# Hybrid decoder trunk: lambda's softplus joined to the decay's log, modulation steps and gated-output splits spread, output-projection weights put into the ordered slots

## Chip, core and metric

The kernel runs on one NeuronCore of one Trainium2 chip. TensorE (PE) does the matrix products, VectorE (DVE), ScalarE (ACT) and GpSimd (POOL) the element-wise work, and SyncE (SP) issues most DMA transfers. The metric is the device time of one execution in microseconds (us).

## What is computed

A trunk of two layers runs over one sequence of 1024 positions of width 1024, in float32. Every layer is `x + gate(c) * mixer(rmsnorm(x) * (1 + scale(c)) + shift(c))`, and a norm follows the last.

```python
mod = c_act @ ada_w[layer] + ada_b[layer]          # shift, scale, gate
# layer 0
log_f = jax.nn.log_sigmoid((f_logit + b_f).astype(jnp.float32))
b_out = forgetting_attention(b_q, b_k, b_v, log_f)  # logits + cumulative log decay
y = jnp.concatenate([a_out, b_out], axis=-1) * jax.nn.silu(gate)
return y @ w_out
# layer 1
log_a = -LRU_C * r * jax.nn.softplus(-lam.astype(jnp.float32))
a = jnp.exp(log_a)
u = jnp.sqrt(-jnp.expm1(2.0 * log_a)) * (i * xc.astype(jnp.float32))
# h_t = a_t h_(t-1) + u_t along the sequence
y = jnp.transpose(hs, (1, 0, 2)).astype(h.dtype) * jax.nn.silu(gate)
return y @ w_out
```

`a_out` is a sliding-window attention of 8 heads; r and i are sigmoids of block-diagonal products of xc, the causal convolution of the first half of the input projection.

## The kernel before

Activations lie transposed: 8 tiles of 128 channels (KT = 8), and two halves of 512 positions, h0 and h1. A float32 product is taken as three products of rounded parts, so every operand is split: `copy` (line 103) rounds it on ACT, and `sub` (112) takes the rest on DVE or POOL. A product of one output tile by one half is a group of 24 matmuls with 512 columns. `split` and `half_of` do this for weights: ACT rounds (whi), POOL takes the rest (wlo).

**Order.** A scheduler may move instructions on an engine unless its name is in the set `ordered` (lines 73 to 97): then they are kept as the code is written. An engine works through its instructions in order, so one that waits holds up those behind it, and SP's transfers behave in the same way.

**Start, gates, modulation.** `squares` makes the norm's sums. `log1p_exp_neg_abs` (153) is the log(1 + exp(-abs(z))) of a softplus or a log-sigmoid; it needs ACT's exp and log tables. The modulation vector is made by 32 steps in the gate loop and after it: `mod_steps` (541) runs one `mod_dot`, an instruction on DVE over 128x1024 numbers of `ada`, and `fetch` loads the following pieces. Pieces come as pairs in a buffer V or alone in a buffer P (line 526).

**V and decay.** The loop over tb (from 614) makes the V tiles of both attentions (`va`, `vb`) and the forget logits `fz`, in PSUM banks that alternate between two pools of two. Then `lf`, the log decay, is made; `sp` and `nsp` are made from lambda by a chain of its own (lines 638 to 643). The first fill (k and q projections of attention A: ak_0, aq_0) follows, with `decay()` (648) at its 48th matmul: it scans `lf` (`loc`) and writes the decays to memory (`gd`). A fill's group is `ps_fill` in a pool of two banks; `use_k` and `use_q` empty it, each half by copies on ACT and subtractions on DVE (`kla`, `aq`).

**Attention.** `weave` (1059) interleaves the units' instructions (scores sA, sB; transposes ptA, ptB, split into pth and ptl; products oA, oB) with a fill of projections for a later unit. In the last fill but one, `then_split` (1125) makes `drip` call `split_act` (1113) six times, which splits the gated outputs gy into yh (ACT) and yl (DVE for odd tiles, POOL for even). They are the operands of layer 0's output projection, the fill after that.

**Layer 1.** `slot(c)` (1422) handles channel tile c: `gates(c)` makes psr and psi, four groups of three matmuls; ACT makes r, i, th, a; DVE the products and the scan hs; then `proj1` of lx_(c+2) for h0 and h1 and of lg_c for h0 and h1, 24 matmuls each. `gate_a` and `gate_b` make y1 = silu(lg) * hs and its split. `split_xc` and `split_r` split the operands of the next slot's gates (xch, xcl; wrh, wrl). `load_next` and `split_next` feed the weights of lx and lg in the order of use; everything here is in program order.

**Output projection.** Behind the slots `ordered` is cleared (1468), and three stretches of positions (512, 256, 256) are multiplied by 8 weight tiles wo. In the first stretch, groups e = 0 to 2 leave out the last input tile until y1 of it is there (AHEAD = 3). Loads and splits of wo stand in the loop over e, and so does the load of x (`xn`, from `x1d`).

Of the kernel before, what the change touches and what calls it, by code (L numbers as in the profile page):

```python
# [48 lines left out]
def hybrid_trunk(  # L49
# [472 lines left out]


    chunks, ndone = {}, [0]
    units = collections.deque()
    for m in range(0, 32, 4):
        units += [(m, m + 1), (m + 2,), (m + 3,)] if m < 24 else [(m + i,) for i in range(4)]
    held = {1: 0, 2: 0}

    def fetch():  # L530

        while units and held[len(units[0])] < 3 - len(units[0]):
            u = units.popleft()
            n = len(u)
            held[n] += 1
            t = at.tile([P, 2, S], F32, tag="V", name=f"ada_{u[0]}") if n == 2 else t4("P", f"ada_{u[0]}").unsqueeze(1)
            sync.dma_start(t, ada[:, u[0] : u[0] + n])
            for i, m in enumerate(u):
                chunks[m] = t[:, i], n if i + 1 == n else 0

    def mod_steps(n):
        for _ in range(min(n, 32 - ndone[0])):
            m = ndone[0]
            lay, c0 = ((0, 16), (1, 0), (1, 8), (1, 16))[m // KT]
            j = c0 + m % KT
            t, n = chunks.pop(m)
            ab = C_AB0 + 24 * lay + j
            mod_dot(t, crow, lay, j, col[:, ab : ab + 1])
            ndone[0] += 1
            if n:  # L550
                held[n] -= 1
            fetch()

    NV = 264
# [59 lines left out]
    z = at.tile([P, NB, 8], F32, tag="fz", name="fz", bufs=1)  # L614
# [20 lines left out]
    lf = at.tile([P, NB, 8], F32, tag="lf", name="lf", bufs=1)  # L635
    log1p_exp_neg_abs(lf, z, at, [P, NB, 8], "sp")
    dve.scalar_tensor_tensor(out=lf, in0=z, scalar=0.0, in1=lf, op0=ALU.min, op1=ALU.subtract)

    sp, nl, nsp = (const.tile([P, KT], F32, name=n) for n in ("sp", "nl", "nsp"))
    lam = col[:, C_LAM : C_LAM + 8]  # L640
    log1p_exp_neg_abs(sp, lam, const, [P, KT], "lm")
    dve.tensor_scalar(out=nl, in0=lam, scalar1=-1.0, scalar2=0.0, op0=ALU.mult, op1=ALU.max)
    add(dve, sp, sp, nl)
    dve.tensor_scalar(out=nsp, in0=sp, scalar1=-8.0, scalar2=None, op0=ALU.mult)
    dve.tensor_scalar(out=sp, in0=sp, scalar1=8.0, scalar2=None, op0=ALU.mult)
    gd = dram.tile([8, NB, S], F32, name="gd")

    def decay():
# [297 lines left out]
    def fill(jobs, ahead=lambda: None):  # L946
# [3 lines left out]
        for n, (_, ks, xs, use) in enumerate(jobs):  # L950
# [5 lines left out]
            for h, (xhi, xlo) in xs().items():  # L956
                ps = ps_mm(f"ps_fill_{h}")
                cnt = 0
                for k in ks:
                    whi, wlo = w[k]  # L960
                    for i, (a, b) in enumerate(((whi, xhi), (wlo, xhi), (whi, xlo))):
                        mm(ps, a, b[:, k], start=(k == ks[0] and i == 0), stop=(k == ks[-1] and i == 2))
                        cnt += 1
                        if late and cnt == 9:
                            late.pop()()
                        if drip and cnt % 4 == 0:
                            drip.popleft()()
                        yield MM
                x = use(h, ps)
# [143 lines left out]
    def split_act(ti, h):  # L1113
# [11 lines left out]
    def then_split(job):  # L1125

        weights, ks, xs, use = job
# [6 lines left out]
        return weights, ks, xs, use_and_split  # L1134

    def residual(xn, ps, lay, e):
        dve.scalar_tensor_tensor(
# [27 lines left out]

    o0 = [o0_job(e) for e in range(KT)]
    jobs.append(o0)
    jobs[7][-1] = then_split(jobs[7][-1])
# [148 lines left out]
    halves = collections.deque((ti, i, name) for ti, name in jobs_l for i in range(2))  # L1317
    raws, ready = collections.deque(), collections.deque()

    def load_next():  # L1320
        if halves:
            ti, i, name = halves.popleft()
            raws.append((load_w(wl[ti][:, 4 * i : 4 * i + 4], [P, 4, P], f"{name}_{i}"), f"{name}_{i}"))

    def split_next():
        if raws:
            w = []
            for _ in range(2):
                w += half_of(raws.popleft())
                load_next()  # L1330
            ready.append(w)

    def rt(tag, c, dt=F32, w=S, bufs=1):
        return rp.tile([P, w], dt, tag=tag, name=f"{tag}_r{c}", bufs=bufs)
# [60 lines left out]
    def gate_a(c, h):  # L1395
# [1 line left out]
        sg = sgs[c, h] = rp.tile([P, HALF], F32, tag="sg", name=f"sg_r{c}_{h}", bufs=2)  # L1397
        act.activation(sg, lgs[c, h], AF.Sigmoid)
        mul(dve, sg, lgs[c, h], sg)
        mul(gp, sg, sg, hss[c][:, half(h)])  # L1400

    def gate_b(c, h):
        sg = sgs.pop((c, h))
        copy(y1h[:, c, half(h)], sg)
        sub(gp, y1l[:, c, half(h)], sg, r32(y1h[:, c, half(h)]))

    lgs, sgs = {}, {}
    ordered |= ALL
# [4 lines left out]
        conv(c, 0, ps01[c])()  # L1413
    split_xc(0, half(0))
    split_r(0)
    taps = conv(0, 1, proj1(0, "lx_0", 1, w01[0]))
    split_next()
    taps()
# [2 lines left out]

    def slot(c):
        n = c + 2
        ps = gates(c)
        if c:
            gate_a(c - 1, 1)
# [14 lines left out]
        w = ready.popleft()  # L1441
        split_next()
        if n < KT:
            taps = conv(n, 0, proj1(0, f"lx_{n}", 0, w))
        act.activation(a2, a_, AF.Square)
        if n < KT:
            taps()
# [17 lines left out]
        slot(c)  # L1465
    gate_a(KT - 1, 1)
    gate_b(KT - 1, 1)
    ordered.clear()
    l1.close()


    xp = ctx.enter_context(tc.tile_pool(name="xp1", bufs=2, reuse_waits="tile"))
    wout = []
    for t0, tw in ((0, 512), (512, 256), (768, 256)):
        h, o = t0 // HALF, t0 % HALF
        ts = slice(t0, t0 + tw)
        xn = xp.tile([P, KT, tw], F32, tag="xn", name=f"x2_{t0}")
        sqa = xp.tile([P, tw], F32, tag="sqa", name=f"sqa2_{t0}")
        late_ = []
        for e in range(KT):  # L1480
            if t0 == 0:
                if e % 4 == 1:
                    wr = [hl.tile([P, 4, KT, P], F32R, tag=f"hl{e // 4 * 2 + i}", name=f"wo1_{e}_{i}") for i in range(2)]
                    for c in range(4):
                        wout.append([(wr[0][:, c, k], wr[1][:, c, k]) for k in range(KT)])
                if e == 0:
                    wout.append(load_tile(wo1[0], "wo1_0"))
                else:
                    for c in range(2):
                        raw = load_w(wo1[e][:, 4 * c : 4 * c + 4], [P, 4, P], f"wo1_{e}_{c}")  # L1490
                        split(raw, *(t[:, (e - 1) % 4, 4 * c : 4 * c + 4] for t in wr))
            w = wout[e]
            sync.dma_start(xn[:, e], x1d[:, h, e, o : o + tw])
            ps = ps_1(f"ps_o1_{t0}_{e}")
# [5 lines left out]
            for e_, w_, ps in late_:  # L1500
# [3 lines left out]
                if t0 < 768 or e_ + 1 < KT:  # L1504
                    square_sum(sqa, xn[:, e_], e_, xp, f"o1_{t0}")
            late_ = []
        sqs = [sqa]
        if t0 == 768:
            sqs.append(xp.tile([P, tw], F32, tag="sq", name=f"sq7_{t0}", bufs=2))
# [84 lines left out]
```

## Time and profile before

| | |
|---|---|
| median of 3 runs | 895.16 us (893.98 to 898.52) |
| profiled execution | 896.32 us, span 894.5 us |
| mean granted TensorE clock | 0.986 |
| PE matmuls | 4618 records, 862.2 us busy |
| DVE, ACT, POOL busy | 563.4, 537.6 and 378.3 us |

The span runs from the first instruction to the last; the rest of the execution's time lies around it. A profile counts an engine as busy while it has an instruction in hand. "Idle before" is the time in which the engine had nothing to run before an instruction, and the releaser is what it waited for. Matmuls of 512 columns start 0.23 us apart although each shows 0.39 us, since they overlap.

### The profile page before, as it was taken

The numbers are of one execution on the slowest core, as the hardware profiler recorded it, in microseconds if no ns is written. First come the engines' busy times: TensorE is split into PE (matmuls) and PEld (weight loads), VectorE is DVE, ScalarE is ACT, GpSimd is POOL, SyncE is SP. The second block draws the span as 40 slices with busy tenths as digits, with TensorE's granted clock in tenths as the row PEclk, the third lists the DMA queues.
The fourth block names the chain that finished last, engine by engine and source line by source line (L and its number), as shares of the span: only waits on it lengthen the run. The fifth ranks groups of instructions, "written<-read, shape, count | busy, mean of one in ns | idle before, by whom it ended". The sixth has DMA issues, their size and how long they took to land.

```text
span 894.5 us, 13516 instructions
## 1 busy us (share of the span) xinstructions
PE 862.2 (96%) x4618; PEld 731.6 (82%) x4618; DVE 563.4 (63%) x1143; ACT 537.6 (60%) x1051; POOL 378.3 (42%) x428
## 2 busy tenths in 40 slices
PE   8999989999999999999999999999999999998995
PEld 8887888888878888888778888877888888777995
DVE  6976797688676566666656768376555566423353
ACT  5756124688676566665666647358767666764332
POOL 3843342343352232331554645532456555773000
PEclk8999999999999999999999999999999999999998
DMA  9933884100113223322463564412111111134042
GB/s 347 414 135 142 263 307 124 42 25 25 36 42 113 88 93 112 121 86 78 132 204 112 176 195 147 140 36 64 43 54 39 44 54 54 48 106 165 3 152 82
DMA packets 54333, 103.83 MB, mean 116 GB/s; under 512 B 6929, under 2 KB 20689, under 8 KB 53497
## 3 DMA queue, kind: packets, MB, share of 16 engines
q1 hardware_dynamic: 53112, 101.93, 34.0%
q10 hardware_dynamic: 1152, 1.05, 0.5%
q8 instruction: 36, 0.59, 0.3%
q14 instruction: 33, 0.26, 0.1%
HBM read 94.02 MB, written 8.93 MB: 115 GB/s over the span
## 4 chain that ended last, share of the span: by engine, by line
PE 62%; DVE 12%; ACT 11%; issue 5%; POOL 4%; DMA 4%; SPq 0%; DVEq 0%; POOLq 0%; ACTq 0%
PE ps_fill L85 21%; PE ps_o L85 8%; PE ps_o0c L85 5%; PE pst L85 5%; PE oB L85 4%; PE ptB L85 3%; PE sB L85 3%; DVE xc_r L85 3%; DMA ada<-in_ada_dram 2%; DVE hs_r L85 2%; PE ps_lx L85 2%; DVE ada L85 2%; PE sA L85 2%; PE oA L85 1%; PE ptA L85 1%
## 5 line engine op out<-in xcount | busy, mean ns | idle before, releaser
L85 PE MATMUL ps_o<-y1h,wo 128*128 128x256 f32 (+1 forms) x336 | 76.3, 323 | 3.9 <-DVE x L85 2.7
L85 DVE TENSOR_TENSOR ptl_B<-ptB,pth_B 128x512 fp32r<-128x512 f32 (+1 forms) x80 | 50.8, 635 | 39.5 <-ACT pth_B L85 39.2
L85 ACT ACTIVATE pth_B<-ptB 128x512 fp32r<-128x512 f32 (+1 forms) x80 | 44.1, 551 | 47.6 <-PE ptB L85 47.4
L85 ACT ACTIVATE pB<-pB,mnB 128x128 f32<-128x128 f32 (+3 forms) x64 | 49.5, 774 | 31.1 <-DVE mnB L85 25.7
L85 PEld LDWEIGHTS ps_o<-y1h,wo 128*128 128x128 f32 x336 | 56.6, 193 | 9.3 <-DVE x L85 3.1
L85 POOL TENSOR_SCALAR_AFFINE_SELECT pB<-pB 128x128 f32<-128x128 f32 x64 | 19.2, 303 | 94.8 <-DMA pB<-gd 84.1
L85 PE MATMUL pst<-hh,ws 128*128 128x512 f32 x192 | 55.3, 396 | 0.0
L85 PE MATMUL ps_o<-y1l,wo 128*128 128x256 f32 (+1 forms) x168 | 53.9, 323 | 0.0
L85 PE MATMUL ps_lx<-h1l,whi_lx 128*128 128x512 f32 x128 | 50.4, 394 | 0.2 <-POOL h1l L85 0.2
L85 PE MATMUL ps_lx<-h1h,whi_lx 128*128 128x512 f32 x128 | 50.5, 395 | 0.0
L85 PE MATMUL ps_lx<-h1h,wlo_lx 128*128 128x512 f32 x128 | 50.3, 393 | 0.0
L85 DVE CUSTOM_DVE_ANT_0 ada<-ada,crow,col 128x1024 f32<-128x1024 f32 x32 | 46.0, 1465 | 6.9 <-DMA ada<-in_ada_dram 6.9
L85 DVE SCALAR_TENSOR_TENSOR xc_r<-ps_lx,col,xc_r 128x509 f32<-128x509 f32 (+2 forms) x48 | 35.6, 744 | 23.2 <-ACT xt_r L85 22.1
L85 PE MATMUL ps_lg<-h1h,whi_lg 128*128 128x512 f32 x128 | 49.8, 389 | 0.0
L85 PE MATMUL ps_lg<-h1l,whi_lg 128*128 128x512 f32 x128 | 49.8, 389 | 0.0
L85 PE MATMUL ps_lg<-h1h,wlo_lg 128*128 128x512 f32 x128 | 49.8, 389 | 0.0
L85 ACT ACT_TABLE_LOAD x37 | 47.5, 1283 | 2.6 <-DVE sq_pth L85 0.9
L85 PE MATMUL ptB<-ident,pB 128*128 128x128 f32 x288 | 45.9, 276 | 3.0 <-DVE gy L85 1.2
L85 PEld LDWEIGHTS ptB<-ident,pB 128*128 128x128 f32 x288 | 35.9, 141 | 14.8 <-ACT pB L85 2.5
L85 DVE CUSTOM_DVE_ANT_0 pB<-sB,pB 128x384 f32<-128x384 f32 (+2 forms) x64 | 35.4, 554 | 17.4 <-PE sB L85 8.2
L85 ACT ACTIVATE sq_o<-x 128x512 f32<-128x512 f32 (+1 forms) x33 | 17.9, 545 | 42.0 <-DVE x L85 41.7
L85 PEld LDWEIGHTS pst<-hh,ws 128*128 128x128 f32 x192 | 35.9, 188 | 8.7 <-issue 0.6
(317 smaller groups left out, 2826.8 us busy)
## 6 DMA issues: line engine op xcount, KB each, us to landing
ada<-in_ada_dram SPq DMA_DIRECT2D x36, 512.0 KB
ada<-in_ada_dram SPq DMA_DIRECT2D x6, 1024.0 KB
x<-in_xT_dram SPq DMA_DIRECT2D x20, 256.0 KB
pB<-gd SPq DMA_DIRECT2D x8, 512.0 KB
raw_o0a<-in_wo_dram SPq DMA_DIRECT2D x16, 256.0 KB
raw_o0c<-in_wo_dram SPq DMA_DIRECT2D x16, 256.0 KB
x1d<-x SPq DMA_DIRECT2D x16, 256.0 KB
raw_lx<-in_wl_dram SPq DMA_DIRECT2D x16, 256.0 KB
```

The lines of the kernel that those rows point to most:

```text
L85: ins = issue(*args, **kw)
```

## The change

Six things are changed.

1. lambda becomes a ninth block of the forget logits (`z[:, NB]`), and `sp` and `nsp` are taken from `lf`'s ninth block. Its own chain goes.
2. Modulation: steps in the gates of h1 become 2 per tile (1 at the last) from 3, in the V stage 1 per block from 1 or 2, and eight steps go into the first fill, one every 12 matmuls. DVE is kept in program order through the V stage and that fill. Pairs end at m = 16.
3. Splits of gated outputs: `drip` fires every 8 matmuls from every 4, the jobs of that fill are arranged q, v(h0), k with the splits, v(h1), and all yl of h0 are made on POOL.
4. lx_2's h0 goes ahead of `gates(0)`.
5. `split_r` of the next slot moves up behind `split_xc`, with its load a slot earlier.
6. Output projection: its weights join the lists of `load_next`; wo_0 and wo_1 are split in slot 7, wo_2 behind the last y1, wo_(e+3) in step e; x is loaded before the loop; e = 0 to 3 use the gates' PSUM banks; tile 7's products and y1l are made on DVE.

```diff
-            if i < 7:
-                mod_steps(3)
+            mod_steps(2 if i < 7 else 1)
...
-    ordered.add("pe")
+    ordered |= {"pe", "dve"}
...
+    z = at.tile([P, NB + 1, 8], F32, tag="fz", name="fz", bufs=1)
+    lam = col[:, C_LAM : C_LAM + 8]
+    gp.tensor_copy(z[:, NB], lam)
...
-        mod_steps(1 + tb % 2)
+        mod_steps(1)
...
-    log1p_exp_neg_abs(sp, lam, const, [P, KT], "lm")
...
+    dve.tensor_scalar(out=nsp, in0=lf[:, NB], scalar1=8.0, scalar2=None, op0=ALU.mult)
+    dve.tensor_scalar(out=sp, in0=lf[:, NB], scalar1=-8.0, scalar2=None, op0=ALU.mult)
...
-                        if drip and cnt % 4 == 0:
+                        if drip and cnt % 8 == 0:
...
+        if n % 12 == 8:
+            mod_steps(1)
+    ordered.discard("dve")
...
-        sub(dve if ti % 2 else gp, yl[h][:, ti], gy[h][:, ti], r32(yh[h][:, ti]))
+        sub(dve if ti % 2 and h else gp, yl[h][:, ti], gy[h][:, ti], r32(yh[h][:, ti]))
...
+        return [jq, part(0), (weights, ks, xs, use_and_split), part(1)]
...
+    jobs_l = [(wl[ti], name) for ti, name in jobs_l] + [(wo1[e], f"wo1_{e}") for e in range(KT)]
...
+    def split_out(e):
...
+        for c in range(2):
+            split(raws.popleft()[0], *(t[:, n % 4, 4 * c : 4 * c + 4] for t in wr))
+            load_next()
...
-        mul(gp, sg, sg, hss[c][:, half(h)])
+        mul(gp if c + 1 < KT else dve, sg, sg, hss[c][:, half(h)])
...
+        if c == 0:
+            w = ready.popleft()
+            ps_x = proj1(0, f"lx_{n}", 0, w)
         ps = gates(c)
...
-            load_r(c + 1)
             split_xc(c + 1)
+            split_r(c + 1)
+            if c + 2 < KT:
+                load_r(c + 2)
...
-        if c + 1 < KT:
-            split_r(c + 1)
+        elif c == KT - 1:
+            wout.append(ready.popleft())
+            split_out(1)
...
+        for e in range(KT):
+            sync.dma_start(xn[:, e], x1d[:, h, e, o : o + tw])
+        if t0 == 0:
+            split_out(2)
...
+            if t0 == 0 and e + 3 < KT:
+                split_out(e + 3)
...
+            ps = (ps_s, ps_t)[e % 2](nm) if t0 == 0 and e <= AHEAD else ps_1(nm)
```

How this stands on two engines is shown at two places.

On DVE, near the end of the first fill, before: `loc` are the decay's scans, `kla` and `aq` the subtractions that empty a fill's bank, and `pA` the first softmax.

```order
204 L85 TENSOR_SCALAR loc<-loc 8x256
205 L85 TENSOR_TENSOR kla_1321<-ps_fill_1379,kha_1319 64x512
206 L85 CAST kha_1319<-kha_1319 64x512
207 L85 TENSOR_SCALAR loc<-loc 8x384
208 L85 TENSOR_SCALAR loc<-loc 8x512
209 L85 TENSOR_SCALAR loc<-loc 8x640
210 L85 TENSOR_SCALAR loc<-loc 8x768
211 L85 TENSOR_SCALAR loc<-loc 8x896
212 L85 SCALAR_TENSOR_TENSOR aq_0_1484<-ps_fill_1424,aq_0_1484 64x512
213 L85 SCALAR_TENSOR_TENSOR aq_1_1485<-ps_fill_1424,aq_1_1485 64x512
214 L85 SCALAR_TENSOR_TENSOR aq_0_1484<-ps_fill_1490,aq_0_1484 64x512
```

The same place on DVE after the change; `ada` with `mod` is a modulation step.

```order
189 L85 TENSOR_SCALAR loc<-loc 8x640
190 L85 TENSOR_SCALAR loc<-loc 8x768
191 L85 TENSOR_SCALAR loc<-loc 8x896
192 L85 ISA ada_1364,mod<-ada_1364,crow,col 128x1024
193 L85 ISA mod 128x1
194 L85 SCALAR_TENSOR_TENSOR gsc<-mod,col 128x8
195 L85 ISA ada_1379,mod<-ada_1379,crow,col 128x1024
196 L85 ISA mod 128x1
197 L85 SCALAR_TENSOR_TENSOR aq_0_1470<-ps_fill_1404,aq_0_1470 64x512
198 L85 SCALAR_TENSOR_TENSOR aq_1_1471<-ps_fill_1404,aq_1_1471 64x512
199 L85 ISA ada_1449,mod<-ada_1449,crow,col 128x1024
200 L85 ISA mod 128x1
```

All `loc` now stand behind the last `kla`, and two modulation steps stand ahead of the first pair of `aq`, two ahead of the second. Four more steps stand further up, between and ahead of the `kla`.

On ACT, at the end of layer 1, before: `a_r` and `th_r` belong to slot 7, `wo` are the output projection's weights, `sg_r` the gates of tile 7.

```order
820 L85 ACTIVATE a_r_8163<-r_r_8156,nsp 128x1024
821 L85 ACTIVATE wo_1_0_8279<-raw_wo_1_0_8281 128x512
822 L85 ACTIVATE wo_1_0_8279<-raw_wo_1_1_8285 128x512
823 L85 ACTIVATE wo_1_0_8279<-raw_wo_2_0_8312 128x512
824 L85 ACTIVATE a_r_8164<-a_r_8163 128x1024
825 L85 ACTIVATE wo_1_0_8279<-raw_wo_2_1_8316 128x512
826 L85 ACT_TABLE_LOAD
827 L85 ACTIVATE th_r_8162<-th_r_8162,tiny 128x1024
828 L85 ACT_TABLE_LOAD
829 L85 ACTIVATE sg_r_0_8201<-ps_lg_0_8176 128x512
830 L85 ACTIVATE wo_1_0_8279<-raw_wo_3_0_8362 128x512
831 L85 ACTIVATE wo_1_0_8279<-raw_wo_3_1_8366 128x512
```

And after the change.

```order
817 L85 ACTIVATE a_r_8157<-r_r_8150,nsp 128x1024
818 L85 ACTIVATE whi_wo_0_0_8164<-raw_wo_0_0_7956 128x512
819 L85 ACTIVATE whi_wo_0_1_8170<-raw_wo_0_1_8060 128x512
820 L85 ACTIVATE a_r_8158<-a_r_8157 128x1024
821 L85 ACT_TABLE_LOAD
822 L85 ACTIVATE th_r_8156<-th_r_8156,tiny 128x1024
823 L85 ACTIVATE wo_1_0_8182<-raw_wo_1_0_8066 128x512
824 L85 ACTIVATE wo_1_0_8182<-raw_wo_1_1_8168 128x512
825 L85 ACT_TABLE_LOAD
826 L85 ACTIVATE sg_r_0_8217<-ps_lg_0_8192 128x512
827 L85 ACTIVATE y1h<-sg_r_0_8217 128x512
828 L85 ACTIVATE sg_r_1_8248<-ps_lg_1_8223 128x512
```

`wo_0` now stands in slot 7 where `wo_1` stood, `wo_1` behind the square root of slot 7, and `wo_2` behind the last y1h, where before the first half of it came ahead of the square of `a_r`.

More of the change, by code (lines that the diff above doesn't have):

```diff
@@ L524, in hybrid_trunk @@
     chunks, ndone = {}, [0]
-    units = collections.deque()
+    blocks = collections.deque()
     for m in range(0, 32, 4):
-        units += [(m, m + 1), (m + 2,), (m + 3,)] if m < 24 else [(m + i,) for i in range(4)]
-    held = {1: 0, 2: 0}
+        blocks += [(m, m + 1), (m + 2,), (m + 3,)] if m < 16 else [(m + i,) for i in range(4)]
+    room = {1: 0, 2: 0}
     def fetch():
-        while units and held[len(units[0])] < 3 - len(units[0]):
-            u = units.popleft()
+        while blocks and room[len(blocks[0])] < 3 - len(blocks[0]):
+            u = blocks.popleft()
             n = len(u)
-            held[n] += 1
+            room[n] += 1
             t = at.tile([P, 2, S], F32, tag="V", name=f"ada_{u[0]}") if n == 2 else t4("P", f"ada_{u[0]}").unsqueeze(1)
@@ L1122, in split_act, with then_split @@
         copy(yh[h][:, ti], gy[h][:, ti])
-        sub(dve if ti % 2 else gp, yl[h][:, ti], gy[h][:, ti], r32(yh[h][:, ti]))
-    def then_split(job):
-        weights, ks, xs, use = job
+        sub(dve if ti % 2 and h else gp, yl[h][:, ti], gy[h][:, ti], r32(yh[h][:, ti]))
+    def then_split(jq, jv, jk):
+        weights, ks, xs, use = jk
         def use_and_split(h, ps):
@@ L1132, in use_and_split, with part @@
                 drip.extend(lambda ti=ti: split_act(ti, 0) for ti in range(KT - 2))
-        return weights, ks, xs, use_and_split
+        def part(h):
+            return (*jv[:2], lambda: {h: (hh[h], hlo[h])}, jv[3])
+        return [jq, part(0), (weights, ks, xs, use_and_split), part(1)]
     def residual(xn, ps, lay, e):
@@ L1316, in hybrid_trunk @@
         jobs_l += [(c + 2, f"lx_{c + 2}")] * (c + 2 < KT) + [(8 + c, f"lg_{c}")]
-    halves = collections.deque((ti, i, name) for ti, name in jobs_l for i in range(2))
+    jobs_l = [(wl[ti], name) for ti, name in jobs_l] + [(wo1[e], f"wo1_{e}") for e in range(KT)]
+    halves = collections.deque((src, i, name) for src, name in jobs_l for i in range(2))
     raws, ready = collections.deque(), collections.deque()
@@ L1321, in load_next @@
         if halves:
-            ti, i, name = halves.popleft()
-            raws.append((load_w(wl[ti][:, 4 * i : 4 * i + 4], [P, 4, P], f"{name}_{i}"), f"{name}_{i}"))
+            src, i, name = halves.popleft()
+            raws.append((load_w(src[:, 4 * i : 4 * i + 4], [P, 4, P], f"{name}_{i}"), f"{name}_{i}"))
     def split_next():
[L1326 to L1331, printed above, removed]
+        w = []
+        for _ in range(2):
+            w += half_of(raws.popleft())
+            load_next()
+        ready.append(w)
+    wout, wr = [], []
+    def split_out(e):
+        n = e - 1
+        if n % 4 == 0:
+            wr[:] = [hl.tile([P, 4, KT, P], F32R, tag=f"hl{n // 4 * 2 + i}", name=f"wo1_{e}_{i}") for i in range(2)]
+        for c in range(2):
+            split(raws.popleft()[0], *(t[:, n % 4, 4 * c : 4 * c + 4] for t in wr))
+            load_next()
+        wout.append([(wr[0][:, n % 4, k], wr[1][:, n % 4, k]) for k in range(KT)])
     def rt(tag, c, dt=F32, w=S, bufs=1):
@@ L1404, in gate_b @@
         copy(y1h[:, c, half(h)], sg)
-        sub(gp, y1l[:, c, half(h)], sg, r32(y1h[:, c, half(h)]))
+        sub(gp if c + 1 < KT else dve, y1l[:, c, half(h)], sg, r32(y1h[:, c, half(h)]))
     lgs, sgs = {}, {}
@@ L1440, in slot @@
         act.activation(a_, r, AF.Exp, scale=nsp[:, c : c + 1])
-        w = ready.popleft()
+        if c:
+            w = ready.popleft()
         split_next()
         if n < KT:
-            taps = conv(n, 0, proj1(0, f"lx_{n}", 0, w))
+            taps = conv(n, 0, proj1(0, f"lx_{n}", 0, w) if c else ps_x)
         act.activation(a2, a_, AF.Square)
@@ L1478, in hybrid_trunk @@
         sqa = xp.tile([P, tw], F32, tag="sqa", name=f"sqa2_{t0}")
+        for e in range(KT):
+            sync.dma_start(xn[:, e], x1d[:, h, e, o : o + tw])
+        if t0 == 0:
+            split_out(2)
         late_ = []
         for e in range(KT):
[L1481 to L1491, printed above, removed]
+            if t0 == 0 and e + 3 < KT:
+                split_out(e + 3)
             w = wout[e]
-            sync.dma_start(xn[:, e], x1d[:, h, e, o : o + tw])
-            ps = ps_1(f"ps_o1_{t0}_{e}")
+            nm = f"ps_o1_{t0}_{e}"
+            ps = (ps_s, ps_t)[e % 2](nm) if t0 == 0 and e <= AHEAD else ps_1(nm)
             last = KT - 1 if t0 == 0 and e < AHEAD else KT
@@ L1506, in hybrid_trunk @@
             late_ = []
+        ordered.clear()
         sqs = [sqa]
```

19 lines of the change are left out of this document (6 added, 13 removed).

## Prediction

> **What bounds the kernel now.** I read the page first, for the busy shares of the engines.
>
> ```profile
> PE 862.2 (96%) x4618; PEld 731.6 (82%) x4618; DVE 563.4 (63%) x1143; ACT 537.6 (60%) x1051; POOL 378.3 (42%) x428
> ```
>
> PE is busy for 96% of the span, and the change neither adds nor removes a matmul. What can be won is therefore PE's idle time and the stretches in which its clock is halved. The waits, with PE as the one who waits, say where that idle time is (total, times, longest):
>
> ```profile
> PE oB L85 <- DVE ptl_B L85: 2.8, 3, 1.6
> PE ps_o L85 <- DVE x L85: 2.7, 1, 2.7
> ...
> PE psr L85 <- ACT xch_r L85: 1.9, 1, 1.9
> PE ps_v L85 <- DVE fz L85: 1.4, 1, 1.4
> ...
> PE ps_v L85 <- POOL wvl L85: 1.1, 1, 1.1
> ...
> PE psr L85 <- POOL wrl_r L85: 0.9, 1, 0.9
> PE psi L85 <- POOL wrl_r L85: 0.7, 1, 0.7
> ```
>
> No wait dominates: the largest is 2.8 us in three pieces. The stretches show what the clock takes besides (length, busy time of the engines, granted clock, DMA share, GB/s):
>
> ```profile
> 10.00:20.00 10.00, 10.00 (x61) 9.91 (x61) 8.31 (x18) 3.39 (x7) 2.51 (x2) 0.66 1.01 386
> 120.00:130.00 10.00, 8.57 (x71) 8.39 (x70) 10.00 (x19) 2.66 (x7) 5.62 (x3) 1.00 0.78 248
> 440.00:450.00 10.00, 8.38 (x41) 6.92 (x41) 7.06 (x17) 5.20 (x11) 3.80 (x8) 0.83 0.06 15
> 600.00:610.00 10.00, 8.12 (x29) 5.96 (x28) 8.18 (x16) 6.55 (x10) 3.54 (x4) 0.85 0.23 66
> 810.00:820.00 10.00, 7.93 (x29) 6.45 (x30) 5.58 (x8) 5.50 (x9) 2.38 (x2) 0.83 0.88 305
> ```
>
> Behind the waits of 1.6 (oB), 1.9 (psr) and 2.7 us (ps_o) the clock falls to 0.83, 0.85 and 0.83 for ten us, which costs 1.7, 1.5 and 1.7 us more; behind the 1.4 us of ps_v it stays at 1.00. So I price an idle stretch of over about 1.6 us at itself plus 1.7. The Trainium skill, "TensorE: Matmul & The Clock Gate", section "Why this matters for your kernels", asks only for no gap of over about 3 us; the three rows speak against it, since shorter gaps were followed by the lower clock, and what it would make of the sum stands with the rivals.
>
> **Start-up.** The softplus of lambda leaves ScalarE's start; its eight columns ride in the decay's log.
>
> ```profile
> 3.38 1.28 ACT L85 ACT_TABLE_LOAD   x1
> 4.68 0.21 ACT L85 ACTIVATE lm<-lm 128x8 f32<-128x8 f32 x1
> 4.91 1.28 ACT L85 ACT_TABLE_LOAD   x1
> ```
>
> Two table loads of 1.28 go, 2.6 us in which the squares of the norm waited. They can't all be won: the DMA is full (1.01 from 10 to 20), the squares need x, and a clock of 0.66 in that stretch is there whether the work starts early or late. Ends 0 and -2.6; I take -1.7, nearer to the loads. What is added (one copy on GpSimd, eight columns more on a 64-column chain) is hidden: GpSimd is 42% busy.
>
> **Modulation steps and the V stage.** DVE is busy for all of 120 to 130, and the writes of va, vb and fz stand behind steps such as this:
>
> ```profile
> 121.52 2.30 DVE L85 CUSTOM_DVE_ANT_0 ada<-ada,crow,col 128x1024 f32<-128x1024 f32 x1
> ```
>
> With fewer steps in the gates and one per V block, the two ps_v waits go: -2.5. But eight steps now lie in the fill of ak and aq, and DVE's order is now the program's there. This is what DVE did in that stretch (138 to 161; busy, mean ns, idle before and releaser), and the last read of a fill's bank:
>
> ```profile
> L85 DVE TENSOR_TENSOR_SCAN loc<-ones,lfT 8x128 f32<-8x128 f32 x8 | 3.3, 411 | 1.0 <-PE lfT L85 0.9
> L85 DVE TENSOR_TENSOR kla<-ps_fill,kha 64x512 fp32r<-64x512 f32 x4 | 2.7, 681 | 1.3 <-ACT kha L85 1.3
> L85 DVE CUSTOM_DVE_ANT_0 ada<-ada,crow,col 128x1024 f32<-128x1024 f32 x2 | 2.6, 1284 | 0.8 <-DMA ada<-in_ada_dram 0.8
> L85 DVE SCALAR_TENSOR_TENSOR aq<-ps_fill,aq 64x512 fp32r<-64x512 f32 x2 | 1.4, 690 | 0.7 <-ACT aq L85 0.7
> ```
>
> ```profile
> 160.32 0.69 DVE L85 SCALAR_TENSOR_TENSOR aq<-ps_fill,aq 64x512 fp32r<-64x512 f32 x1 [0.66 <-ACT aq L85]
> ```
>
> ```profile
> 161.16 0.47 PE L85 MATMUL ps_fill<-hh,whi_aq 128*128 128x512 f32 x1
> ```
>
> The aq subtraction ends at 161.01, and PE begins the next fill, which takes the same bank, at 161.16: no slack already. In the new order six more steps (the moved ones 24 to 29) stand ahead of that subtraction, as do all scans and all TENSOR_SCALARs of loc. Six by 1.28 is 7.7 us; of this DVE can put 1.0 + 1.3 + 0.8 + 0.7 = 3.8 into its old idle times. So PE waits 3.9 us, and 1.7 for the clock: +5.6. Ends: 0, if DVE leaves the V stage so much earlier that it catches up, and 7.7 + 1.7. Queued behind are loc's writes, and on SP the last two ada loads behind those. Together -2.5 + 5.6 = +3.1.
>
> **Splits of the gated outputs.** The burst before PE's 1.6 us of oB:
>
> ```profile
> L85 ACT ACTIVATE yh<-gy x6: 619/623/624, 434.8 to 437.8; 128x512 fp32r<-128x512 f32 x6
> L85 POOL TENSOR_TENSOR yl<-gy,yh x2: 1293/1521/1749, 435.5 to 436.7; 128x512 fp32r<-128x512 f32 x2
> L85 DVE TENSOR_TENSOR yl<-gy,yh x2: 1315/1342/1370, 435.9 to 437.7; 128x512 fp32r<-128x512 f32 x2
> ```
>
> The two of about 1.34 on DVE go to GpSimd, where the row says 1.29 to 1.75, so they are no slower there and free DVE. The six copies on ACT stay in one place: four, one khb, two, and only then the pth_B that PE wants next. Ends: the 1.6 + 1.7 goes (-3.3), or ACT's 3.7 us of copies keep as long a wait (0). I take -1.2, nearer to staying. A later subtraction of the same kind, which moves off DVE ahead of the third, 1.0 us wait of oB (2.8 less 1.6 is what the other two hold), gives 0 to -1.0: -0.5.
>
> **Layer 1 and the output projection.** These edits meet in ScalarE's chain, so I follow that.
>
> ```profile
> 603.02 0.40 PE L85 MATMUL psr<-xch_r,wrh_r 128*128 128x512 f32 x1
> ```
>
> ```profile
> 607.69 1.26 ACT L85 ACTIVATE r_r<-psr,col 128x512 f32<-128x512 f32 x2
> ```
>
> ```profile
> 614.54 1.14 ACT L85 ACTIVATE whi_lg<-raw_lg 128x512 fp32r<-128x512 f32 x2
> ```
>
> ```profile
> 615.29 1.29 POOL L85 TENSOR_TENSOR wlo_lg<-raw_lg,whi_lg 128x512 fp32r<-128x512 f32 x1 [11.23 <-issue]
> ```
>
> ```profile
> 746.54 0.50 ACT L85 ACTIVATE wrh_r<-wr_r 128x128 fp32r<-128x128 f32 x2
> ```
>
> A group of 24 products in these rows takes 24 x 0.23 = 5.5 us. With lx_2's first half ahead of the gates, PE fills its 1.9 us (and the clock's 1.5), but the first psr ends at 603.0 + 5.5 + 0.7 = 609.2, so r_r comes 1.7 late. With 0.4 of wrh now ahead of it, whi_lg comes at 616.7 and GpSimd's first half of wlo_lg ends at 615.29 + 1.29 + 2.1 = 618.7; PE wants it at 603.0 + 5.5 + 2.7 + 5.5 = 616.7. Of the 3.4 removed 2.0 come back at once. From then on ScalarE's loop of a slot is longer by about 0.3 (the 0.4, with 0.1 of slack), and over six slots it takes the rest; the 0.9 + 0.7 of the weights' low halves goes (-1.6).
>
> ```profile
> 783.58 1.66 ACT L85 ACTIVATE wo<-raw_wo 128x512 fp32r<-128x512 f32 x3
> ```
>
> ```profile
> 784.68 0.39 PE L85 MATMUL ps_o<-y1h,whi_wo 128*128 128x512 f32 x1
> ```
>
> ```profile
> 812.07 0.80 PE L85 MATMUL ps_o<-y1h,wo 128*128 128x512 f32 x1 [2.72 <-DVE x L85]
> ```
>
> ```profile
> 792.64 2.29 DVE L85 TENSOR_TENSOR_SCAN hs_r<-a_r,i_r 128x1024 f32<-128x1024 f32 x1
> ```
>
> ```profile
> 811.26 2.12 DVE L85 SCALAR_TENSOR_TENSOR x<-ps_o,mod,x 128x512 f32<-128x512 f32 x3 [8.46 <-DMA x<-x1d]
> ```
>
> wo_0 is now split where wo_1 was: 783.6, plus 1.7 + 0.4 + 1.7 of lag, less about 2 since GpSimd's part of wo_0 no longer stands ahead of the gate of the slot before: about 785.6. A copy and GpSimd's 1.29 later, at 787.5, the first low half is there. PE is ready at 784.7 - 1.6 = 783.1, so it waits 4.4 us. wo_2 comes in ScalarE's order only behind the last y1h. The last scan ended at 794.9 and I leave it there (the lag against the three wo copies that no longer stand ahead of it); sigmoids, two products and y1h of both halves then take about 4 us and wo_2's copy and low half 1.9: about 800.6, and till then the third group waits. From there 21, 24 and 9 products (12.4 us) end at 813.0. Before, the fifth group began at 812.1, at half clock (1.7): worth 813.8. x is loaded early, so the 2.7 us wait for it goes, as does its clock. Layer 1 and the projection: -0.8; ends -7 (3.4 + 1.6 + 4.4 gone, 2.0 back, ScalarE doesn't lag) and +4 (the low clock behind both new waits).
>
> **Sum.** -1.7 + 3.1 - 1.2 - 0.5 - 0.8 = -1.1. The profiled execution took 896.32 us (span 894.5 and 1.8 around it), 1.2 above the median of 895.16. So 895.2 by it, and 894.0 as a median.
>
> **The rivals.** One: the removed waits go and nothing takes their place. Then 2.6 + 2.5 + 3.3 + 1.0 + 3.4 + 1.6 + 4.4 = 18.8 go, 876.4. Against it: the aq bank without slack. If that wait alone stays out, it is 894.0 - 5.6 = 888.4, so this case spans 876 to 889. For it: DVE idles in the fill, and it gets there with less behind it.
>
> Two, on the slower side: DVE, in program order, blocks the fill for longer. If all eight steps cost 2.30, as beside GpSimd at 121.52, and each waits for its load for 0.4, as two did for 0.8, this adds 8 x 1.02 + 3.2 = 11.4: 905.4. It decides the sign from a wait of about 9.5 at the bank, 5.6 over mine. For it: two buffers hold all that is loaded ahead, and SP has loc's writes ahead of the last loads. Against: GpSimd is busy for 42% of the span, so most steps would not run beside it.
>
> Three: the clock doesn't follow from short waits. Then the 1.7 given to oB's and the projection's gaps isn't won, and the sum is -1.1 + 1.7 + 1.7 = +2.3, a median of 897.4. This is what the rule of the Trainium skill's page above would give, since only the 3.9 us at the bank is over its bound.
>
> **How the numbers follow.** The forecast has 0.45, with 889 to 899 of its own; the first rival 0.30, the second 0.18, the third 0.07. A measurement of this kernel tells about 0.5% from no change, 890.7 and 899.6. Faster: 0.28 of the first rival and 0.09 of the forecast, 0.37. Slower: 0.18 + 0.04 + 0.02 = 0.24. The same: 0.39. The range leaves out the ends of the first two rivals: 880 to 902.
>
> **What would show it.** The fill: PE waiting for aq by 3 to 5 us near 160, with DVE at a modulation step; without that wait the forecast is too slow. ScalarE's first squares come over 2 us earlier, and PE has no ps_v wait. In layer 1 a wait of ps_lg for wlo_lg near 617, none of psr for xch_r, and near 782 and 798 waits of ps_o for wo's low halves where there was one for x. If ps_o waits for nothing, ScalarE's lag was wrong.

## The result, and the profile after

The changed kernel takes 908.25 us (median of 4 runs, 906.54 to 911.03), the kernel before 895.23 us (4 runs, 893.98 to 898.52). The ratio is 1.0143, with an interval of 1.0105 to 1.018: slower, where no change was forecast, and above the range. The profiled execution of the changed kernel took 907.82 us, with a span of 905.7 us, 11.2 more than before, and a mean granted clock of 0.977.

The busy shares of the engines after the change, from the page:

```profile
PE 867.2 (96%) x4618; PEld 735.4 (81%) x4618; DVE 564.4 (62%) x1134; ACT 535.0 (59%) x1047; POOL 372.7 (41%) x429
```

This row shows nothing of what happened: every engine has as much work as before, within 1.5%. The waits of PE after the change (total, times, longest) show it:

```profile
PE ps_fill L85 <- DVE aq L85: 6.5, 1, 6.5
PE ps_fill L85 <- DVE kla L85: 3.8, 1, 3.8
PE ps_o L85 <- ACT whi_wo L85: 3.5, 1, 3.5
PE rs_n L85 <- DVE vb_n L85: 2.9, 4, 1.8
PE ps_o L85 <- ACT wo L85: 2.4, 1, 2.4
PE oB L85 <- ACT pth_B L85: 1.7, 2, 1.4
PE ps_lg L85 <- ACT whi_lg L85: 1.6, 1, 1.6
```

The waits of ps_v, of psr and of ps_o for x are gone from it. At the head stand two waits of ps_fill, both for a subtraction on DVE that empties a bank, and then two for the output projection's weights. The stretches around them (length, busy time of PE, PEld, DVE, ACT, POOL, granted clock, DMA share, GB/s):

```profile
110.00:120.00 10.00, 10.00 (x84) 9.92 (x83) 3.99 (x10) 3.63 (x8) 6.51 (x5) 1.00 0.80 261
...
140.00:150.00 10.00, 6.18 (x27) 4.43 (x26) 7.95 (x14) 4.74 (x8) 4.26 (x4) 0.84 0.48 150
150.00:160.00 10.00, 10.00 (x40) 8.06 (x39) 8.43 (x18) 1.77 (x3) 2.75 (x3) 0.82 0.45 132
160.00:170.00 10.00, 3.50 (x15) 2.62 (x14) 9.09 (x13) 2.33 (x4) 3.19 (x2) 0.86 0.48 134
170.00:180.00 10.00, 10.00 (x42) 8.19 (x41) 5.23 (x14) 4.20 (x10) 0.19 (x1) 0.80 0.11 40
...
790.00:800.00 10.00, 5.67 (x18) 4.03 (x17) 4.01 (x3) 9.00 (x12) 4.41 (x4) 0.83 0.16 52
800.00:810.00 10.00, 7.36 (x30) 5.28 (x28) 7.58 (x8) 5.04 (x8) 5.47 (x3) 0.95 0.49 157
810.00:820.00 10.00, 9.72 (x31) 7.81 (x32) 1.43 (x2) 1.89 (x3) 6.49 (x6) 0.71 0.92 313
```

From 110 to 120 PE is full and DVE idles for 6.0 of 10 us; from 140 to 150 and from 160 to 170 it is the other way round, DVE is at 8.0 and 9.1 and PE idles, and the mean clock of each of the four stretches to 180 lies between 0.80 and 0.86. In slices of 1 us it is 0.50 from 147 to 153 and from 168 to 174, and 1.00 from 154 to 167. A second, smaller hole lies at 790 to 820.

To see where the 11.2 us arise, one takes the time at which the first matmul of a stage starts, in both traces:

| first matmul of | before | after | later by | gained or lost in the stage ahead |
|---|---|---|---|---|
| the gates (pst) | 19.98 | 17.47 | −2.5 | start-up −2.5 |
| the V stage (ps_v) | 111.86 | 110.08 | −1.8 | gates +0.7 |
| the first fill (ps_fill) | 138.18 | 133.42 | −4.8 | V stage −3.0 |
| the first scores (sA) | 165.34 | 175.75 | +10.4 | **first fill +15.2** |
| layer 1 (ps_lx) | 577.81 | 585.64 | +7.8 | attention, with the splits −2.6 |
| lg of the first slot (ps_lg) | 620.71 | 626.35 | +5.6 | start of layer 1 −2.2 |
| lg of the last slot | 773.77 | 779.42 | +5.6 | the slots 0 |
| the output projection (ps_o) | 784.68 | 793.99 | +9.3 | into the projection +3.7 |
| the end of the span | 894.5 | 905.7 | +11.2 | projection +1.9 |

Four of the stages gain, 10.3 us in all, and the first fill alone takes 15.2. What DVE did there after the change (133.4 to 170; busy, mean ns, idle before and its releaser), in groups:

```profile
L85 DVE CUSTOM_DVE_ANT_0 ada<-ada,crow,col 128x1024 f32<-128x1024 f32 x9 | 13.6, 1532 | 0.1
L85 DVE TENSOR_SCALAR loc<-loc 8x128 f32<-8x128 f32 (+6 forms) x7 | 4.3, 609 | 0.3
L85 DVE TENSOR_TENSOR_SCAN loc<-ones,lfT 8x128 f32<-8x128 f32 x8 | 3.3, 410 | 0.1
L85 DVE TENSOR_TENSOR kla<-ps_fill,kha 64x512 fp32r<-64x512 f32 x4 | 2.7, 687 | 2.5 <-ACT kha L85 2.5
```

Nine steps reach into this stretch (seven of the eight in the fill, and two of the V stage), where the prediction's view of before had two, and they take 1.53 us on the mean. The idle time ahead of kla has not shrunk, it has grown from 1.3 to 2.5. In order of time on DVE (start, duration):

```profile
143.28 2.31 DVE L85 CUSTOM_DVE_ANT_0 ada<-ada,crow,col 128x1024 f32<-128x1024 f32 x1
...
147.45 0.69 DVE L85 TENSOR_TENSOR kla<-ps_fill,kha 64x512 fp32r<-64x512 f32 x1 [1.26 <-ACT kha L85]
...
150.08 2.28 DVE L85 CUSTOM_DVE_ANT_0 ada<-ada,crow,col 128x1024 f32<-128x1024 f32 x1
...
158.95 4.50 DVE L85 TENSOR_SCALAR loc<-loc 8x128 f32<-8x128 f32 x7
163.48 1.28 DVE L85 CUSTOM_DVE_ANT_0 ada<-ada,crow,col 128x1024 f32<-128x1024 f32 x1
...
164.69 1.22 DVE L85 SCALAR_TENSOR_TENSOR gsc<-mod,col 128x8 f32<-128x8 f32 x1
...
168.49 0.69 DVE L85 SCALAR_TENSOR_TENSOR aq<-ps_fill,aq 64x512 fp32r<-64x512 f32 x1 [0.66 <-ACT aq L85]
```

And PE at the two banks:

```profile
148.29 0.77 PE L85 MATMUL ps_fill<-hh,whi_aq 128*128 128x512 f32 x1 [3.82 <-DVE kla L85]
...
169.32 0.77 PE L85 MATMUL ps_fill<-hh,whi_aq 128*128 128x512 f32 x1 [6.50 <-DVE aq L85]
```

The second kla ends at 148.14 and PE goes on at 148.29; the second aq ends at 169.18 and PE goes on at 169.32. Ahead of the first stand two modulation steps (142.07 to 145.5), ahead of the second the scans, all of loc, two more steps and gsc. The matmul behind each takes 0.77 us and the next ones start 0.43 us apart, where they took 0.39 and started 0.23 apart: that is the clock of 0.50.

### The profile page after: what moved, and what is told of

Same layout as the page of the kernel before. It is cut to its first block, busy times and chain, and to the rows that moved or that the text cites. A ratio compares the mean times of both kernels' runs of the same rounds, so it can differ in the third digit from the quotient of the medians.

```text
span 905.7 us, 13502 instructions
## 1 busy us (share of the span) xinstructions
PE 867.2 (96%) x4618; PEld 735.4 (81%) x4618; DVE 564.4 (62%) x1134; ACT 535.0 (59%) x1047; POOL 372.7 (41%) x429
## 4 chain that ended last, share of the span: by engine, by line
PE 59%; DVE 13%; ACT 11%; issue 6%; DMA 6%; POOL 3%; SPq 1%; ACTq 0%; DVEq 0%; POOLq 0%
PE ps_fill L85 20%; PE ps_o L85 9%; PE pst L85 5%; PE ps_o0c L85 5%; PE oB L85 4%; PE sB L85 4%; PE ptB L85 3%; DVE xc_r L85 2%; DMA ada<-in_ada_dram 2%; DVE ada L85 2%; DVE hs_r L85 2%; PE sA L85 2%; PE ps_lx L85 1%; ACT th_r L85 1%; PE ps_lg L85 1%
## 5 line engine op out<-in xcount | busy, mean ns | idle before, releaser
L85 DVE CUSTOM_DVE_ANT_0 ada<-ada,crow,col 128x1024 f32<-128x1024 f32 x32 | 44.0, 1397 | 10.7 <-DMA ada<-in_ada_dram 10.6
L85 PEld LDWEIGHTS ptB<-ident,pB 128*128 128x128 f32 x288 | 35.7, 140 | 11.8 <-PE rbT_B L85 1.4
L85 POOL TENSOR_TENSOR wlo_lx<-raw_lx,whi_lx 128x512 fp32r<-128x512 f32 x16 | 30.7, 1933 | 29.0 <-ACT whi_lx L85 27.5
```

What stands on the lines that cost most here:

```text
L85: ins = issue(*args, **kw)
```

## The experiments

**The theories.** A: the loss comes from the modulation steps that now lie in the first fill, and the rest of the change is about neutral. B, its rival: it comes from another part. Within A, two more are told apart: A1, the program order on DVE is what costs; A2, the steps' work in that stage is.

**Part 2 undone (e1).** The steps lie in the gates and the V stage again, DVE is free there, and all else is as changed.

```diff
-            mod_steps(2 if i < 7 else 1)
+            if i < 7:
+                mod_steps(3)
...
-    ordered |= {"pe", "dve"}
+    ordered.add("pe")
...
-        mod_steps(1)
+        mod_steps(1 + tb % 2)
...
-        if n % 12 == 8:
-            mod_steps(1)
-    ordered.discard("dve")
```

> The changed kernel with its modulation part undone (steps and engine order through the V stage and the first fill as before), all else as changed. Theory A (the loss is made in the first fill, by the steps that DVE keeps in program order): PE's two waits there, 3.8 and 6.5 us, and the low clock behind them go, the two V waits of 2.5 us come back, so about 15 less and 2.5 more: 895 to 897. Theory B (the loss is made in layer 1 and the projection, by ScalarE's lag): 904 to 908.

Measured: 896.46 us, ratio 1.0019 (1.0006 to 1.0032), 11.8 below the changed kernel. The first scores start 0.9 us earlier than before, not 10.4 later. Its waits of PE:

```profile
PE ps_o L85 <- ACT whi_wo L85: 3.6, 1, 3.6
...
PE ps_o L85 <- ACT wo L85: 1.8, 1, 1.8
...
PE ps_v L85 <- POOL wvl L85: 1.5, 1, 1.5
PE ps_v L85 <- DVE fz L85: 1.4, 1, 1.4
```

Both waits of ps_fill are gone (0.2 us is left), and both of ps_v, 2.9 us, are back. So part 2 exchanged 2.9 us of waits in the V stage for 10.3 in the fill. A holds for the larger share of the loss. B does not explain it, but its parts are not neutral in themselves: what all the other parts win by layer 1's first lg, 5.4 us by the first matmuls, is given back at the projection's weights.

**DVE free in the fill (e2).** The same eight steps, but DVE is released from the program's order ahead of the fill.

```diff
+    ordered.discard("dve")
...
             mod_steps(1)
-    ordered.discard("dve")
```

> The changed kernel with the same eight steps in the first fill, but DVE released from program order there. Theory A1 (the order costs, since work that waits for ACT holds up the steps and the steps hold up the emptying of banks): PE's waits in the fill fall from 10.3 to under 3 us, 893 to 898. Theory A2 (eight steps are too much work for DVE in that stretch whatever the order): waits of 6 us or more stay, 902 to 908.

Measured: 904.74 us, ratio 1.0098 (1.0072 to 1.0123). Only 3.5 us are won by the medians, and the intervals of the two ratios overlap. PE's waits show that the hole stays and changes its name:

```profile
PE ps_fill L85 <- DVE kla L85: 4.4, 1, 4.4
PE lfT L85 <- DVE lf L85: 4.3, 1, 4.3
```

The aq wait is gone, but the log decay lf, on which the transposes lfT wait, now comes late instead. DVE also waits twice for a load of ada here, 4.1 us, and the second of these waits, 1.8 us at 142, holds up lf. A1 alone doesn't carry the loss.

**Half as many steps in the fill (e3).** Twelve steps in the V stage as before, four in the fill, DVE in program order.

```diff
-        mod_steps(1)
+        mod_steps(1 + tb % 2)
...
-        if n % 12 == 8:
+        if n % 24 == 20:
```

> The changed kernel with 12 steps in the V stage (one and two by turns, as before) and four in the fill, one in each group of 24 matmuls, DVE in program order. Theory A1: the fixed idle times of the order stay and three to four steps of 1.3 to 2.3 us go from ahead of the last emptying, so the waits fall from 10.3 to about 4 us with one or two stretches of low clock, 898 to 901. Theory A2: about half the steps, so no overload, waits under 1 us, 892 to 895. In both the V waits may come back by up to 2.5 us.

Measured: 902.93 us, ratio 1.0077 (1.005 to 1.0103). Neither number came out. The kla wait grew to 5.5 us and the aq wait shrank to 2.7: the last step of the V stage ends 3.3 us later (140.7 for 137.4), so DVE enters the fill with that much left to do. Work moved from inside the fill to just ahead of it comes back at the first bank.

**Parts 4 to 6 undone (e4).** Layer 1 and the projection as before; the fill as changed.

```diff
-        if c == 0:
-            w = ready.popleft()
-            ps_x = proj1(0, f"lx_{n}", 0, w)
...
-            split_r(c + 1)
...
-        if t0 == 0:
-            split_out(2)
...
+                if e == 0:
+                    wout.append(load_tile(wo1[0], "wo1_0"))
```

> The changed kernel with everything behind layer 0 as before (parts 4 to 6 undone). By the trace the changed kernel is 7.8 us behind at the first product of layer 1 and 11.2 at the end, so these parts cost 3.4: 904 to 906. If the prediction's -0.8 were right for them: 909.

Measured: 902.43 us, ratio 1.0081 (1.0053 to 1.0108), 5.8 below the changed kernel and below what was expected. Those parts cost 5.8 us by the medians and 3.4 by the traces of before and after (+11.2 at the end less +7.8 at layer 1's start), where the prediction had −0.8. That they cost something is clear, the size is not: e4's four runs spread from 901.23 to 905.70, and its interval just overlaps that of the changed kernel.

**No steps in the fill (e5).** DVE is in program order as in the changed kernel, but the last eight steps and their loads are left out, with layer 1's gate set to 0: that part of the computation is missing.

```diff
+    gp.memset(mod[:, 1, 16:24], 0.0)
...
-        for _ in range(min(n, 32 - ndone[0])):
+        for _ in range(min(n, 24 - ndone[0])):
...
-        if n % 12 == 8:
-            mod_steps(1)
```

> The changed kernel with the last eight modulation steps left out (layer 1's gate is set to 0), so that no step stands in the first fill; DVE stays in program order there. Theory A1 (the order alone makes the waits, since the decay's log with its waits for ACT stands ahead of kla): PE still waits for over 4 us in the fill, 899 to 903. Theory A2 (the work of the steps makes them): waits under 1 us, 890 to 893.

Measured: 895.46 us, ratio 1.0006 (0.9986 to 1.0025), 12.8 below the changed kernel. The time lies between the two theories, nearer to A2. Of the two waits one is left:

```profile
PE ps_fill L85 <- DVE aq L85: 2.3, 1, 2.3
```

```profile
150.00:160.00 10.00, 7.67 (x35) 6.06 (x34) 8.29 (x16) 3.83 (x7) 2.46 (x2) 1.00 0.17 41
160.00:170.00 10.00, 10.00 (x54) 8.54 (x53) 4.51 (x17) 6.29 (x18) 1.62 (x7) 1.00 0.09 28
```

So the order alone, with all of loc ahead of aq, costs a wait of 2.3 us and no clock; the eight steps, with their loads, cost 12.8. A2 is the larger share by far.

**Three steps in the gates again (e6).** The gates as before, one step per V block, four in the fill, DVE free in the fill, so that DVE has no idle stretch behind the gates and half the steps in the fill.

```diff
-            mod_steps(2 if i < 7 else 1)
+            if i < 7:
+                mod_steps(3)
...
+    ordered.discard("dve")
...
-        if n % 12 == 8:
+        if n % 24 == 20:
```

> The changed kernel with three steps per gate tile again, one per V block, and the last four in the fill with DVE free in its order there. Theory A2 in its sharper form (steps were taken out of a stretch in which DVE then idled 14 us, and put where DVE sets the pace): 20 steps are done ahead of V, DVE enters the fill little behind PE, its waits there are under 2 us, and the V waits stay below 2.5: 893 to 897. If the order made the loss, as 896.5 of the kernel without the modulation part shows too, this is no better than that: 896 to 899.

Measured: 901.72 us, ratio 1.0082 (1.0054 to 1.011). This missed. PE waits 5.0 us for kla, 1.5 for lf and 2.3 for wvl, and now DVE itself waits for its data, 2.6, 2.5 and 1.5 us. Its loads, on SP:

```profile
126.48 19.52 SPq L85 DMA_DIRECT2D ada<-in_ada_dram  x7
```

The seven pieces that are left at 126 go out over 19.5 us, since a buffer for the next comes free only behind a step. In the changed kernel that row is much the same (eight pieces over 24.6 us from 121), but there seven of the steps of the fill wait 0.1 us for loads together, and the eighth waits 1.9 us at 172, when PE no longer waits. So there it is DVE's work; here it is the loads too.

**The projection's weights a slot earlier (e7, again as e11).** e1's kernel, with wo_0 split at the end of slot 6, wo_1 in slot 7 where the change has wo_0, and wo_2 behind slot 7's square root.

```diff
-        split_next()
+        if c + 1 < KT:
+            split_next()
+        else:
+            split_out(1)
...
-            wout.append(ready.popleft())
-            split_out(1)
+            split_out(2)
...
+        if c == KT - 2:
+            split_next()
...
+        if c == KT - 1:
+            wout.append(ready.pop())
...
-        if t0 == 0:
-            split_out(2)
```

> The kernel without the modulation part (896.5), with wo_0 split at the end of slot 6, wo_1 in slot 7 where the changed kernel has wo_0, and wo_2 behind the square root. Theory (the projection's two waits for wo, 3.6 + 0.6 and 1.8 + 0.9 us, with the low clock behind them, come from their places in ScalarE's order): they go, 888 to 891. Rival (y1 of the last tile is late anyway, and the products for it wait instead): 893 to 897.

> The kernel without the modulation part and with wo_0, wo_1 and wo_2 split early, a second time with more rounds: 887 to 889, 0.7 to 0.9% below the kernel before.

Measured: 888.06 us, ratio 0.9925 (0.9902 to 0.9948), and again 889.93 us, 0.9944 (0.9925 to 0.9963). The first lies in its range and the second just above its own. It beats both kernels: 5 to 7 us below before, 18 to 20 below the changed one. The same stretches of its projection, and the row of waits of ps_o that is left (another has 0.3 us):

```profile
780.00:790.00 10.00, 9.79 (x43) 7.52 (x41) 4.68 (x4) 8.97 (x11) 4.96 (x4) 1.00 0.24 75
790.00:800.00 10.00, 7.78 (x32) 5.50 (x31) 8.40 (x9) 4.75 (x8) 5.47 (x4) 1.00 0.53 172
800.00:810.00 10.00, 10.00 (x44) 8.31 (x45) 2.31 (x4) 4.80 (x8) 6.67 (x5) 1.00 0.93 310
```

```profile
PE ps_o L85 <- POOL wo L85: 2.1, 4, 0.9
```

The waits are now four short ones, none above 0.9 us, and the clock stays at 1.00, where e1 has 0.66 at 780 to 790. The 6.5 to 8.4 us between e1 and this kernel are e1's four waits of 3.6, 0.6, 1.8 and 0.9 (6.9, less the 2.1 that stay) and the clock behind them.

**Only wo_2 earlier (e10).** e1's kernel with wo_2 ahead of the last y1h.

```diff
+            split_out(2)
...
-        if t0 == 0:
-            split_out(2)
```

> The kernel without the modulation part (896.5) with wo_2 alone moved, from behind the last y1 to behind wo_1 and the square root; wo_0 stays in slot 7. Theory (both waits for wo cost by themselves): the wait of 1.8 + 0.9 us goes and the one for wo_0 of 3.6 + 0.6 stays, 893 to 894. Rival (the first wait only delays PE to where the second would have ended anyway): 889 to 891 or no change at 896.

Measured: 891.14 us, ratio 0.9962 (0.9944 to 0.998), 5.3 below e1, more than expected: the time is at the edge of the rival's range. The trace shows the theory's waits and not the rival's: the wait for wo_0 stays at 3.6 us with a clock of 0.71 behind it, the one for the third group is gone, and so is the low clock that came with it.

**e6 and e7 together (e8).** The edits of both.

```diff
-        if n % 12 == 8:
+        if n % 24 == 20:
...
-            split_out(1)
+            split_out(2)
```

> The two edits before this one together: the sum of their gains, 885 to 890 if both theories hold.

Measured: 895.69 us, ratio 1.0008 (0.999 to 1.0025). It missed: the projection is as in e7, but waits of 2.2 us for kla, 1.8 for lf and 2.3 for wvl stay, with a clock of 0.83 from 110 to 120 and of 0.66 from 150 to 160.

**Part 1 alone (e9).** The kernel before, with lambda as the ninth block.

```diff
-    z = at.tile([P, NB, 8], F32, tag="fz", name="fz", bufs=1)
+    z = at.tile([P, NB + 1, 8], F32, tag="fz", name="fz", bufs=1)
...
-    log1p_exp_neg_abs(sp, lam, const, [P, KT], "lm")
```

> The kernel before with part 1 alone (lambda's softplus in the decay's log). Theory from the landmarks of the kernels run so far (first gate product 1.7 to 2.5 us earlier, 1.2 to 1.6 left at the end of V): 893.5 to 894.5 where before is 895. Rival (the whole of the two table loads stays): 892.5.

Measured: 894.23 us, ratio 0.9995 (0.9976 to 1.0014), not to be told from no change. In the trace the gates start 2.9 us earlier, the first fill 0.4 and the first scores 0.1: what the start wins, the V stage gives back, where PE waits 2.3 us for wvl in place of 1.1, with a clock of 0.83 behind it that wasn't there. PE reaches that stage 2.1 us earlier and waits 1.2 longer, so the weights' low halves come only 0.9 earlier.

## Why the prediction was wrong

**Start-up** (−1.7). By the start of the gates −2.5, close to the whole of the two table loads. Alone it is worth nothing at the end, since the V stage's waits take it back (e9).

**The V stage** (−2.5). Right: both ps_v waits go, and the stage is 3.0 us shorter.

**The first fill** (+5.6). This step failed, and it alone turns the result: it took 15.2. The sentence that fails is "of this DVE can put 1.0 + 1.3 + 0.8 + 0.7 = 3.8 into its old idle times". In program order a step runs only at its own place: DVE waited 2.5 us for kha and 0.7 for aq and did nothing meanwhile (whether the piece of the next step had landed by then isn't shown), and 0.8 of the 3.8 had itself been a wait for a modulation piece. Four things were left out besides. The order alone, priced at nothing, costs a wait of 2.3 us (e5). The six steps ahead of the aq that PE waits for took 9.9 us and not 7.7, since two of them ran at 2.3 and one at 1.52, beside GpSimd. The kla bank, the first to be taken again, was not looked at; its two steps are 3.6 us, its wait 3.8. And the low clock was priced once, while it came behind both waits: of the 15.2, 10.3 are waits and the other 4.9 are what the lower clock leaves, nearly three times the 1.7. The second rival named what happened: DVE in program order blocks the fill for more than 9.5 us (10.3 at two banks), for 905.4 us. Its loads are not the reason, though, since the steps ahead of the two banks waited 0.1 us for them, and what it left out, the repeated low clock, is why the time is above even that.

How much DVE had to spare was also misread. The prediction allowed that DVE leaves the V stage earlier and catches up. It does leave it earlier, but the steps taken out of the gates left it idle there, 6.0 of the 10 us from 110 to 120, where before it was full: the time was not saved, only shifted to where PE needs DVE.

**The splits** (−1.7). By the traces −2.6 from the scores to layer 1, the right sign but not for the reason given. The waits of oB, on which both terms rested, only shrink from 3.3 to 2.7 us (for ptl_B and pth_B together), and the clock is 0.83 from 440 to 450 as before; what went are 2.3 us of ptB, for gy and pB, while 0.9 of rbT_B came. No run did this part alone.

**Layer 1 and the projection** (−0.8). By the traces +3.4, by e4 +5.8. Up to the last lg it was better than foretold, −2.2 for −1.6, and ScalarE's loop, which was to give the gain back over six slots, gave back nothing: PE has no wait there. The 1.6 us of the weights' low halves did go, but the first lg's second wait (0.8, for wlo_lg) and the low clock behind it (0.90 and 0.93 from 620 to 640) took that back. The wait of the first group was foretold as 4.4 us and measured as 3.5 and 0.85, and the third group waits where it was said to. The term that was mis-sized is what follows these waits: the low clock behind both, 0.83, 0.95 and 0.71 in the three stretches from 790 to 820 (1.7, 0.5 and 2.9 us), stood only in the upper end and not in the sum, although the prediction's own rule priced every wait over 1.6 us with 1.7. e7 shows both sides: with the three splits earlier the waits and the low clock go, and 6.5 to 8.4 us with them.

**The clock.** The third rival took the rule of the Trainium skill, "TensorE: Matmul & The Clock Gate", section "Why this matters for your kernels" (no gap of over about 3 us). The rival said that only the 3.9 us at the bank lie over this bound, but the 4.4 us that the sum expected for wo_0 do too. The runs here speak against it as a bound: the 1.8 us wait of the third group in e1 and the 2.4 in the changed kernel are followed by 0.86 and 0.71, though both are below 3 us. They don't give another bound either, and not the prediction's 1.6 us, since behind the 2.3 us of e5 the clock stays at 1.00, and behind the 2.3 us in e9 it falls to 0.83. The clearest row is one wait of oB for pth_B, which is 1.41 to 1.43 us long in every kernel with part 3: the clock falls behind it in the changed kernel, e3, e4, e6, e10 and e11, and stays at 1.00 in e1, e2, e5, e7 and e8. The wait and the stretch behind it in the changed kernel:

```profile
439.23 0.45 PE L85 MATMUL oB<-pth_B,vb 128*128 128x256 f32 x2 [1.43 <-ACT pth_B L85]
```

```profile
440.00:450.00 10.00, 10.00 (x47) 8.49 (x48) 7.00 (x17) 4.72 (x11) 6.69 (x10) 0.83 0.10 34
```

The same in e1:

```profile
427.85 0.44 PE L85 MATMUL oB<-pth_B,vb 128*128 128x256 f32 x2 [1.41 <-ACT pth_B L85]
```

```profile
430.00:440.00 10.00, 9.90 (x54) 8.27 (x54) 7.79 (x20) 6.15 (x14) 5.95 (x9) 1.00 0.22 53
```

So two profiles can differ by some 1.7 us (0.17 of ten microseconds) with the same wait in both. The same page, in "What's actually happening", says that the window in which activity is counted runs freely. Then the same gap could fall on either side, which would fit these rows, but no run moved a gap within a window on purpose, so it is only argued.

**What stays open.** Whether any order of the steps ends the V stage's waits without a new one in the fill: four were tried (the change, e2, e3, e6), and all lose to leaving them where they were. What the longer steps beside GpSimd cost at the end (2.3 of the 9.9 us) was read from the trace and not tried by itself.

## What to carry to other kernels

An engine's idle time can be filled only from where the work stands in its order, so before work is moved on an engine that also empties another's banks, list which bank is taken again first and what stands ahead of the instruction that empties it. A stage that waits a little for an engine is cheaper than a stage in which that engine is the bound: moving 2.9 us of waits here made 10.3. Of an operand that is split just in time, move the split a stage earlier than the row of its wait suggests, and price the low clock behind a wait in the sum and not only in the range.

## What the runs showed of the hardware that was not expected

- Gaps on PE of 1.6 to 2.4 us were followed by a clock of 0.71 to 0.90 over ten microseconds (1.6 and 0.8 near 620 to 630: 0.90; 2.4 near 809: 0.71), but a single one of 2.3 us in e5 was not (1.00), and one of 1.4 us was in six kernels and was not in five.
- A modulation step of 128x1024 on DVE took 1.28 us alone and up to 2.31 where it met a subtraction or a copy on GpSimd: the two ran one after the other. On GpSimd in the first fill after the change (start, duration):

```profile
142.56 1.94 POOL L85 TENSOR_TENSOR wlo_aq<-raw_aq,whi_aq 128x512 fp32r<-128x512 f32 x1 [22.36 <-ACT whi_aq L85]
...
149.15 2.13 POOL L85 TENSOR_TENSOR wlo_aq<-raw_aq,whi_aq 128x512 fp32r<-128x512 f32 x1
...
160.97 1.35 POOL L85 TENSOR_TENSOR wlo_aq<-raw_aq,whi_aq 128x512 fp32r<-128x512 f32 x1 [5.00 <-PE ps_fill L85]
...
164.05 1.84 POOL L85 TENSOR_TENSOR wlo_aq<-raw_aq,whi_aq 128x512 fp32r<-128x512 f32 x1 [1.73 <-ACT whi_aq L85]
```

Beside no step the subtraction takes 1.35 us. The first ends at 144.50; the step that was next on DVE at 143.28 ends at 145.59, 1.09 after it, and the step of 150.08 ends at 152.36, 1.08 after the second (151.28). The `gsc` of 128x8 numbers that is next at 164.69 takes 1.22 us and ends at 165.91, when the fourth subtraction does (165.89). So each runs for nearly its whole time alone. In e5, which has no steps in the fill, the subtractions there take 1.28 to 1.54 us, and `gsc`, with GpSimd idle, 0.17. That agrees with the Trainium skill, "SBUF — State Buffer", section "Who interferes with whom", by which the port that both share is an exclusive lock and the loser fully blocks; no run was made to test that by itself.
